# A transformer block on one core: one shared tile pool for projection, merging and feed-forward, and the first up-projection operands prepared during the last output projection

## The chip, the cores and the metric

The kernel runs as one program on one core of a Trainium2 chip. The metric is the device time of one execution in microseconds (us). Tensors are float32 in and out. The engines are named as in the profile: PE (matrix multiply, PEld its weight loads), DVE (vector), ACT (scalar and activation), POOL (GpSimd), SP (issues the DMAs). Each works through its own instruction stream in order and waits on semaphores for the others.

## The reference, cut to what matters

One encoder block on 2048 tokens of width 1024. The parts that the change touches are the last lines.

```python
h  = rmsnorm(x, norm1_g)
z  = h @ w_in + b_in                       # q, k, v, two conv inputs, two gates
br_a = neighbourhood_attention(q, k, v, rpb) @ w_na_out
br_b = silu(layernorm(dwconv31(glu))) @ w_conv_out
merged = sigmoid(g_a) * br_a + sigmoid(g_b) * br_b
x  = x + merged @ w_out                    # output projection
h2 = rmsnorm(x, norm2_g)
up = dwconv3(h2 @ w_up) + ffn_dw_b         # 1024 -> 2 * 2816
x  = x + (gelu(gate) * val) @ w_down       # 2816 -> 1024
return rmsnorm(x, norm_f_g)
```

## The kernel before, in words

Every matrix product is made at float32 accuracy out of three matmuls in a rounded 32-bit format: an operand is split into a high part (ACT copies it, line 93) and a low part (DVE subtracts the high part from it, line 94), and high x high, high x low and low x high are summed in PSUM.

Phase A (lines 663 to 733) computes the input projection, the depthwise convolution, the layer norms and the attention. Phase B (`phase_b`, lines 735 to 868) takes four quarters of 512 tokens. For each quarter `merged` makes the gated sum of the two branches in eight blocks of 128 channels (eight input tiles `Z` and eight results `M`, in sixteen `act` buffers), and then four output projections of 128 tokens follow (`tt` 0 to 3, lines 834 to 861, 48 matmuls each, written line 842). Behind each projection DVE adds the residual (line 851), SP stores x2, ACT sums the squares (line 130), POOL makes the reciprocal root in eight small operations (lines 110 to 124), and DVE scales the row (line 854). For the last two projections of quarter 3 SP stores the scaled row to `yn` (line 861).

`h2_tiles` turns finished scaled rows into the rows that the up-projection reads: PE transposes (line 891), ACT scales them (line 892), and in the odd quarters POOL makes four differences per block of channels (line 898) out of this quarter's rows and those of the quarter before, which SP loads back as `hb` (line 889). The seven combinations B11, B21, T1 to T4 and B22 go to `hc` in DRAM. The last block of tokens of quarter 3 is done later, inside the first up-projection (`h2_late`, units 4 to 7).

Phase F runs up-projection half 0, down-projection 0, up-projection half 1, down-projections 1 to 3. The up-projection uses a seven-product scheme: per pair of output blocks (a unit) seven weight combinations A11, S1, S2, A12, S3, S4, A22 (sums made by POOL at lines 955 to 963, split by ACT and DVE) meet the seven row combinations; a product is twelve matmuls (line 985). `duo` handles units 0 and 1 together, because the row combinations are loaded and split on the way: `h_tile` loads 256 KB into one of four `hraw` buffers and splits it into a tile of the `h0` to `h3` groups.

Three things order the work. In phase A the order on PE is the program's own; everywhere else the framework's scheduler places instructions into each engine's stream when their operands and buffers are due, so a load can be placed ahead of its place in the program text when its buffer is free. A tile waits for the last use of whatever lay at its address. And a pool is opened after the pool before it on the same memory has been closed: `wp` and `ap` (phases A and B) are closed before `fp` and `fps` (phase F) are opened.

```python
        with ExitStack() as outer:
            self.wp = pool(outer, "w", 2)
            self.ap = pool(outer, "act", NACT)
```

```python
            sums = [self.w_sums(self.w_raws(0)), None]
            for name in ("A11", "S1"):
                self.w_split(W[0], sums[0], name)
            build("B11")
            A.append(self.bank())
            self.product(A[0], W[0], "A11", H, "B11", first=True)
            s1.append(snap(A[0]))
            sums[1] = self.w_sums(self.w_raws(1))
            build("T1")
```

Of the kernel before, what the change touches and what calls it, by code (L numbers as in the profile page):

```python
# [12 lines left out]
F32 = mybir.dt.float32  # L13
# [35 lines left out]
NACT = 16  # L49
NRAW = 3  # L50
# [5 lines left out]
PAD_ACT, PAD_H = 256, 960  # L56
F_RAW, F_W, F_U, F_C, F_BLK, F_SNAP, F_H = 4, 9, 3, 2, 4, 5, (8, 8, 6, 6)
# [5 lines left out]
BUFS_B = {"gt": 2, "x": 4, "l": 6, "lv": 1, "h2": 3, "hb": 2, "hd": 2, "y": 1}  # L63
# [19 lines left out]
class Block:  # L83
# [12 lines left out]
    def split_weights(self, raw):  # L96
        wh = self.wp.tile([128, 8, 128], F32R, name="wh", tag="wh")
        wl = self.wp.tile([128, 8, 128], F32R, name="wl", tag="wl")
        self.split(wh, wl, raw)
        return wh, wl  # L100

    def raw(self, *shape):
        return self.wp.tile(list(shape) or [128, 8, 128], F32, name="wraw", tag="wraw", bufs=NRAW)
# [559 lines left out]
    def phase_a(self):  # L663
# [5 lines left out]
        def acts(pool, w):  # L669
            return [[pool.tile([128, w], F32R, name="act", tag="act") for _ in range(KC)] for _ in range(2)]  # L670

# [6 lines left out]
        with self.tc.manual_schedule(engines={mybir.EngineType.PE}):  # L678
            with self.pool("x0", 16) as xp, self.pool("xt", 4) as self.xt:
                self.pad(xp, PAD_ACT)  # L680
                tile = lambda: self.ap.tile([128, 1024], F32, name="act", tag="act")[:, :D]
                xs = [self.x_tiles(0, 4, tile)]
                X0 = acts(xp, 1024)
# [8 lines left out]
                for c, raw in zip((16, 12), raws):  # L692
                    w = ws[c] = [self.wp.tile([128, 8, 128], F32R, name=n, tag=n) for n in ("wh", "wl")]
# [11 lines left out]
                X1 = acts(self.ap, 1024)  # L705
# [29 lines left out]
    def phase_b(self):  # L735
# [20 lines left out]
        def load_z(qd):  # L756
# [3 lines left out]
            for src in (self.at, self.cs):  # L760
                for kc in range(4):
                    t = self.ap.tile([128, 1024], F32R, name="act", tag="act")
# [28 lines left out]
        def merged(qd, Z, M):  # L791
            for d in range(8):
# [18 lines left out]
                m = self.ap.tile([128, 1024], F32R, name="act", tag="act")  # L811
# [9 lines left out]
        def main():  # L821
# [5 lines left out]
            for qd in range(4):  # L827
                M, xs = [], []
                yield from merged(qd, Z, M)
                if qd < 3:  # L830
                    Z = load_z(qd + 1)
                load_x(qd * 4)
                load_x(qd * 4 + 1)
                for tt in range(4):
# [20 lines left out]
                    xs.append(x)  # L855
                    if tt < 2:
# [25 lines left out]
    def h2_step(self, kc, e, t0, xs, ps, st, b0, t2):  # L882
# [42 lines left out]
    def k4(self, name, tag, bufs, shape=(128, 1024), dtype=F32):  # L925
        return self.fp.tile(list(shape), dtype, name=name, tag=tag, bufs=bufs)

# [3 lines left out]
    def h_tile(self, H, half, name, kc):  # L931

        r = self.k4("hraw", "hraw", 4, (128, 512))
        self.nc.sync.dma_start(r, self.hc[half, kc, H_AT[name]])
# [3 lines left out]
        self.split(t[:, 0], t[:, 1], r)  # L938
# [10 lines left out]
    def w_sums(self, raws):  # L949

        ra, rb = raws
        s = self.k4("ws", "ws", 2, (128, 2, 4, 128))
# [14 lines left out]
    def w_split(self, W, sums, name):  # L967
        t = W[name] = self.k4("w", "w", F_W, (128, 2, 4, 128), F32R)
# [4 lines left out]
    def w_side(self, raws):  # L973

        sums, W = self.w_sums(raws), {}
# [16 lines left out]

    def phase_up(self, half):
        nc = self.nc
        H = {}
# [70 lines left out]
        def duo():  # L1066

            W, A, E, s1, s5, s2, ua, ub = [{}, {}], [], [], [], [], [], [], []
            build = lambda name: [self.h_tile(H, half, name, kc) for kc in range(4)]
            sums = [self.w_sums(self.w_raws(0)), None]  # L1070
            for name in ("A11", "S1"):
                self.w_split(W[0], sums[0], name)
            build("B11")
            A.append(self.bank())
            self.product(A[0], W[0], "A11", H, "B11", first=True)
            s1.append(snap(A[0]))
            sums[1] = self.w_sums(self.w_raws(1))
            build("T1")
            E.append(self.bank())
            self.product(E[0], W[0], "S1", H, "T1", first=True)  # L1080
            s5.append(snap(E[0]))
# [3 lines left out]
            A.append(self.bank())  # L1085
            self.product(A[1], W[1], "A11", H, "B11", first=True)
            s1.append(snap(A[1]))
            E.append(self.bank())
            self.product(E[1], W[1], "S1", H, "T1", first=True)
            s5.append(snap(E[1]))  # L1090
# [40 lines left out]

        tail = duo()
        wr = {f: self.w_raws(f) for f in (2, 3)}
        Ws = {2: self.w_side(wr.pop(2))}
        for f in range(2, NF):
            if f + 1 < NF:
                Ws[f + 1] = self.w_side(wr.pop(f + 1))
# [7 lines left out]
    def phase_down(self, g):  # L1145
# [67 lines left out]
    def layout(self):  # L1213

        unused = lambda tag, bufs, shape=(128, 1024): self.k4("place", tag, bufs, shape)
        unused("raw", F_RAW)
        unused("ws", 2)
        self.edge = self.fp.tile([128, 124, 2], F32, name="edge")
        unused("w", F_W)
        unused("snap", F_SNAP, (128, 512))  # L1220
        unused("u", F_U, (128, 1083))
        unused("c", F_C, (128, 1027))
        self.pad(self.fp, PAD_H)
        unused("hraw", 4, (128, 512))
        unused("h0", F_H[0])
# [96 lines left out]
```

## Time and profile before

| what | value |
|---|---|
| median of three runs (lowest to highest) | 2808.43 us (2805.88 to 2808.47) |
| the profiled execution's own time | 2805.53 us |
| its span, first to last instruction | 2803.7 us |
| mean granted TensorE clock | 0.989 of 2.4 GHz |
| PE busy | 2715.3 us, 97% of the span |
| DVE / ACT / POOL busy | 1886.3 / 1185.6 / 555.4 us |
| moved by DMA | 463.68 MB, mean 165 GB/s |

The profiled execution lies 1.8 us above its span and 2.9 us (0.1%) below the median. A row of a timeline gives the start and the length of a run of like instructions, the engine, the line, the operation, what it writes and reads, the count, and in brackets how long the engine had been idle and what ended that. A row of waits gives the total, the number and the longest. A window row gives for each engine the busy time and count, then the granted clock, the DMA share and the GB/s.

### The profile page before, as it was taken

Reading aid. Unit: us, or ns where it says so; the run is one execution under the profiler, and the core shown is the slowest. Engines: PE = TensorE matmul, PEld = TensorE weight load, DVE = VectorE, ACT = ScalarE, POOL = GpSimd, SP = SyncE. Lnnn points to the kernel's source line nnn. Section 1 sums busy time; section 2 is a strip of 40 time slices with the busy share of each in tenths; the row PEclk is TensorE's granted clock in tenths of the full one; section 3 lists DMA queues with packets and bytes.
Section 4 is the critical chain, followed back from the end, with each engine's and each line's share of the span. In section 5 each row is a group of like instructions: output and inputs, shape, how many; then the busy total and the mean of one; then the engine's idle time right before and its main releaser. Section 6 shows DMA issues by size and latency. Waiting matters only on the chain.

```text
span 2803.7 us, 34637 instructions
## 1 busy us (share of the span) xinstructions
PE 2715.3 (97%) x12597; PEld 2247.2 (80%) x12597; DVE 1886.3 (67%) x2636; ACT 1185.6 (42%) x1880; POOL 555.4 (20%) x731
## 2 busy tenths in 40 slices
PE   7998999999999999999969999999999999999998
PEld 6787788888888887887858788888888888888887
DVE  4697999668777646756528877875587778734252
ACT  6422222246555543422325555463454555533231
POOL 1101000000000000132043555430444344002021
PEclk9999999999999999999989999999999999999999
DMA  5357733489788868767545342236522222556361
GB/s 176 99 143 235 266 121 117 135 226 253 211 236 230 225 194 288 220 217 233 188 159 168 114 123 83 83 123 209 162 93 83 89 77 83 170 176 216 120 218 53
DMA packets 427704, 463.68 MB, mean 165 GB/s; under 512 B 27041, under 2 KB 336013, under 8 KB 426509
## 3 DMA queue, kind: packets, MB, share of 16 engines
q1 hardware_dynamic: 427533, 461.47, 52.9%
q8 instruction: 99, 1.62, 0.2%
q14 instruction: 72, 0.59, 0.1%
HBM read 336.81 MB, written 141.05 MB: 170 GB/s over the span
## 4 chain that ended last, share of the span: by engine, by line
PE 75%; DMA 9%; issue 6%; DVE 5%; POOL 2%; ACT 2%; SPq 1%; ACTq 0%; POOLq 0%; DVEq 0%
PE bank L985 26%; PE bank L1178 17%; PE mm L297 7%; PE mm L295 7%; PE mm L299 7%; PE ot L614 2%; PE s L569 2%; PE pt L595 2%; PE mm L842 1%; DMA bd<-rext 1%; DMA gt<-gs 1%; SPq L216 1%; DMA hraw<-hc 1%; DMA y<-ys 1%; PE mm L802 1%
## 5 line engine op out<-in xcount | busy, mean ns | idle before, releaser
L985 PE MATMUL bank<-h,w 128*128 128x512 f32 x3696 | 847.0, 391 | 26.2 <-ACT h L93 22.4
L985 PEld LDWEIGHTS bank<-h,w 128*128 128x128 f32 x3696 | 695.1, 188 | 174.1 <-ACT h L93 23.8
L1178 PE MATMUL bank<-wd,g 128*128 128x512 f32 x2112 | 479.7, 389 | 0.0
L295 PE MATMUL mm<-act,wh 128*128 128x512 f32 x1152 | 460.2, 399 | 14.9 <-ACT qt L342 8.7
L1178 PEld LDWEIGHTS bank<-wd,g 128*128 128x128 f32 x2112 | 396.5, 188 | 82.2
L297 PE MATMUL mm<-act,wh 128*128 128x512 f32 x1152 | 461.2, 400 | 0.0
L299 PE MATMUL mm<-act,wl 128*128 128x512 f32 x1152 | 458.4, 398 | 0.2 <-DVE wl L94 0.2
L444 DVE SCALAR_TENSOR_TENSOR acc<-u,dw,acc 128x1008 f32<-128x1008 f32 (+1 forms) x240 | 310.9, 1296 | 5.8
L94 DVE TENSOR_TENSOR w<-wraw,w 128x512 fp32r<-128x512 f32 x220 | 206.9, 953 | 106.5 <-ACT w L93 106.2
L295 PEld LDWEIGHTS mm<-act,wh 128*128 128x128 f32 x1152 | 218.7, 190 | 56.2 <-ACT qt L342 9.9
L299 PEld LDWEIGHTS mm<-act,wl 128*128 128x128 f32 x1152 | 218.8, 190 | 37.0 <-DVE wl L94 0.7
L297 PEld LDWEIGHTS mm<-act,wh 128*128 128x128 f32 x1152 | 218.6, 190 | 36.1 <-DVE act L250 0.3
L94 DVE TENSOR_TENSOR wd<-draw,wd 128x1024 fp32r<-128x1024 f32 x88 | 107.0, 1222 | 177.0 <-ACT wd L93 176.5
L93 ACT ACTIVATE w<-wraw 128x512 fp32r<-128x512 f32 x220 | 135.9, 626 | 164.7 <-PE bank L985 132.6
L93 ACT ACTIVATE wh<-wraw 128x1024 fp32r<-128x1024 f32 x102 | 107.9, 1058 | 211.1 <-PE mm L297 165.7
L93 ACT ACTIVATE wd<-draw 128x1024 fp32r<-128x1024 f32 x88 | 93.2, 1060 | 206.9 <-DMA draw<-in_w_down 151.2
L1016 DVE SCALAR_TENSOR_TENSOR c<-u,fw,c 128x1023 f32<-128x1023 f32 (+1 forms) x88 | 131.7, 1496 | 62.1 <-ACT c L1015 61.6
L94 DVE TENSOR_TENSOR wl<-wraw,wh 128x1024 fp32r<-128x1024 f32 x102 | 126.5, 1241 | 51.9 <-ACT wh L93 47.3
L842 PE MATMUL mm<-woh,act 128*128 128x512 f32 x512 | 142.8, 396 | 2.6 <-DVE gt L809 2.6
L1244 POOL MEMSET pad<- 128x1 f32 x4 | 0.4, 128 | 728.2 <-PE s L569 727.9
L1015 ACT ACTIVATE c<-u,cols,fw 128x1023 f32<-128x1023 f32 (+1 forms) x88 | 109.5, 1245 | 64.7 <-DVE c L1030 37.0
L124 POOL TENSOR_SCALAR v<-ms 128x1 f32<-128x1 f32 x36 | 10.5, 291 | 628.7 <-ACT junk L130 314.6
(169 smaller groups left out, 3831.8 us busy)
## 6 DMA issues: line engine op xcount, KB each, us to landing
wraw<-in_w_up SPq DMA_DIRECT2D x88, 512.0 KB
draw<-in_w_down SPq DMA_DIRECT2D x88, 512.0 KB
wraw<-in_w_in SPq DMA_DIRECT2D x72, 512.0 KB
graw<-gd SPq DMA_DIRECT2D x44, 512.0 KB
gs<-gate SPq DMA_DIRECT2D x64, 256.0 KB
q<-qs SPq DMA_DIRECT2D x64, 256.0 KB
v<-vs SPq DMA_DIRECT2D x128, 128.0 KB
gt<-gs SPq DMA_DIRECT2D x32, 512.0 KB
```

Of the source, the lines that this page charges most:

```text
L93: self.nc.scalar.activation(hi, src, AF.Copy)
L94: self.nc.vector.tensor_tensor(lo, src, hi.bitcast(F32), op=ALU.subtract)
L295: mm(ps, wh[:, kc], X[kc][:, 0:512], start=kc == 0, stop=False)
L297: mm(ps, wh[:, kc], X[kc][:, 512:1024], start=False, stop=False)
L299: mm(ps, wl[:, kc], X[kc][:, 0:512], start=False, stop=kc == KC - 1)
L444: tap = nc.vector.scalar_tensor_tensor(acc, u[:, k : k + n], w(k), acc, ALU.mult, ALU.add)
L569: nc.tensor.matmul(ps[:, :w], q[:, s * 512 + rt * 128 : s * 512 + rt * 128 + 128], kv[:, r0 : r0 + nr, st : st + 32], start=s == 0, stop=s ...
L842: mm(ps[:, nh], l, r[kc][:, nh * 512 : nh * 512 + 512], start=kc == 0 and l is mh and r is woh, stop=kc == KC - 1 and l is ml,)
L985: self.nc.tensor.matmul(ps, w[:, x, kc], h[:, y], start=first and kc == 0 and i == 0, stop=kc == 3 and i == 2, skip_group_check=True,)
L1015: nc.scalar.activation(c, u[:, 1 : 1 + n], AF.Identity, scale=tap(1), bias=self.col(C_FFB, ch))
L1016: nc.vector.scalar_tensor_tensor(c, u[:, 0:n], tap(0), c, ALU.mult, ALU.add)
L1178: mm(ps[tt][nh], x[:, tok], y[:, c], start=f == 0 and i == 0, stop=f == NF - 1 and i == 2,)
```

## The change

It replaces the pools `wp` and `ap` by one pool `ep` that stays open over all phases. `ep` holds four raw buffers (phases A and B had three of their own), five weight buffers `w` (before: two pairs), one buffer `ws0` for sums, and the groups `h0` and `h1` of eight tiles, which serve as the `act` tiles of phases A and B and as row tiles of the up-projection. A new generator `early` loads the raw weights of units 0 and 1 and the row combinations B11 and T1 and makes the splits that the first two products of unit 0 read; in half 0 it is stepped inside the last quarter of phase B, in half 1 it is run through at the start. The `hraw` buffers go: a row combination is loaded into the low half of its tile and split in place. The weights of a unit are divided over two groups of five, `w` and `w1`, where one group of nine served. Three of the four differences of `h2_step` become DVE operations that read PSUM, the fourth a DVE subtraction; POOL makes none. The layer-norm buffers of phase B go from six to five, and the small pads that set addresses get new sizes.

```diff
-F_RAW, F_W, F_U, F_C, F_BLK, F_SNAP, F_H = 4, 9, 3, 2, 4, 5, (8, 8, 6, 6)
+F_RAW, F_W, F_U, F_C, F_BLK, F_SNAP, F_H = 4, (5, 5), 3, 2, 4, 5, (8, 8, 6, 6)
...
-BUFS_B = {"gt": 2, "x": 4, "l": 6, "lv": 1, "h2": 3, "hb": 2, "hd": 2, "y": 1}
+BUFS_B = {"gt": 2, "x": 4, "l": 5, "lv": 1, "h2": 3, "hb": 2, "hd": 2, "y": 1}
...
+    def k4(self, name, tag, bufs, shape=(128, 1024), dtype=F32):
+        pool = self.ep if tag in ("raw", "w", "ws0", "h0", "h1") else self.fp
+        return pool.tile(list(shape), dtype, name=name, tag=tag, bufs=bufs)
+
+    def act(self, j, dtype=F32R):
+        return self.k4("act", f"h{j}", 8, dtype=dtype)
...
                 yield from merged(qd, Z, M)
+                early = self.early(0) if qd == 3 else iter(())
                 if qd < 3:
                     Z = load_z(qd + 1)
+                next(early, None)
                 load_x(qd * 4)
...
                     xs.append(x)
+                    next(early, None)
                     if tt < 2:
...
-        sub = lambda o, x, y: nc.gpsimd.tensor_tensor(o, x, y, op=ALU.subtract)
+        def less(out, e, y):
+            x = ps[:, e * 256 : e * 256 + 256]
+            nc.vector.scalar_tensor_tensor(out, x, self.col(C_G2, kc + 4 * e), y, ALU.mult, ALU.subtract)
+
         t2 = t2[:, 0]
-        sub(b0[:, 0], st[:, 0], b0[:, 0])
-        sub(t2, st[:, 1], b0[:, 0])
-        sub(st[:, 0], st[:, 1], st[:, 0])
-        sub(b0[:, 1], b0[:, 1], t2)
+        less(b0[:, 0], 0, b0[:, 0])
+        less(t2, 1, b0[:, 0])
+        less(st[:, 0], 1, st[:, 0])
+        nc.vector.tensor_tensor(b0[:, 1], b0[:, 1], t2, op=ALU.subtract)
...
-    def h_tile(self, H, half, name, kc):
-
-        r = self.k4("hraw", "hraw", 4, (128, 512))
-        self.nc.sync.dma_start(r, self.hc[half, kc, H_AT[name]])
+    def h_load(self, H, half, name, kc):
+
...
         t = H[name, kc] = self.k4("h", shape=(128, 2, 512), dtype=F32R, **self.h_tag(j))
-        self.split(t[:, 0], t[:, 1], r)
+        self.nc.sync.dma_start(t[:, 1].bitcast(F32), self.hc[half, kc, H_AT[name]])
+
+    def h_split(self, t):
+        self.split(t[:, 0], t[:, 1], t[:, 1].bitcast(F32))
...
     def w_split(self, W, sums, name):
-        t = W[name] = self.k4("w", "w", F_W, (128, 2, 4, 128), F32R)
+        j = name in ("S4", "S3", "A22")
+        t = W[name] = self.k4("w", "w1" if j else "w", F_W[j], (128, 2, 4, 128), F32R)
...
+    def early(self, half):
+
+        H, W, raws = {}, [{}, {}], [self.w_raws(f) for f in range(2)]
+        self.begun = H, W, raws, []
+        first = [(name, kc) for name in ("B11", "T1") for kc in range(4)]
+        for x in first:
+            self.h_load(H, half, *x)
+        yield
+        sums = self.w_sums(raws[0], 0)
+        self.begun[3].append(sums)
+        for name in ("A11", "S1"):
+            self.w_split(W[0], sums, name)
+        yield
+        for x in first[:4]:
+            self.h_split(H[x])
+        yield
+        for x in first[4:]:
+            self.h_split(H[x])
+        yield
...
+            def heads(i):
+                for ps, snaps, a, b in ((A, s1, "A11", "B11"), (E, s5, "S1", "T1")):
+                    ps.append(self.bank())
+                    self.product(ps[i], W[i], a, H, b, first=True)
+                    snaps.append(snap(ps[i]))
+
+            heads(0)
+            sums.append(self.w_sums(raws[1], 1))
             for name in ("A11", "S1"):
                 self.w_split(W[1], sums[1], name)
             build("T2")
...
+            heads(1)
             both = lambda name: [self.w_split(W[i], sums[i], name) for i in range(2)]
...
+        if half:
+            for _ in self.early(half):
+                pass
+        H, W, raws, sums = self.begun
         tail = duo()
...
-                    gh = self.k4("g", "w", F_W, (128, 2, 512), F32R)
-                    gl = self.k4("g", "w", F_W, (128, 2, 512), F32R)
+                    gh, gl = [
+                        self.k4("g", "w1" if j else "w", F_W[j], (128, 2, 512), F32R)
+                        for j in ((f + i) // 2 % 2 for i in range(2))
+                    ]
...
-        with ExitStack() as outer:
-            self.wp = pool(outer, "w", 2)
-            self.ap = pool(outer, "act", NACT)
-            self.pad(self.ap, PAD_ACT)
...
+        self.ep = pool(ctx, "shared", 1)
```

## Rows read from the trace of the kernel before

**Rows 1.** PE's waits, whole run: total us, times, longest us.

```profile
PE bank L985 <- ACT h L93: 22.4, 3, 19.8
...
PE mm L806 <- DVE wl L94: 3.1, 4, 1.9
...
PE bank L985 <- DVE h L94: 2.8, 3, 2.4
...
PE bank L891 <- DMA late<-yn: 2.5, 1, 2.5
```

**Rows 2.** PE's timeline between output projection and up-projection.

```profile
1438.85 0.60 PE L891 MATMUL pt<-ident,x 128*128 128x128 f32 x4
1459.25 3.88 PE L985 MATMUL bank<-h,w 128*128 128x512 f32 x7 [19.80 <-ACT h L93]
...
1483.56 46.77 PE L985 MATMUL bank<-h,w 128*128 128x512 f32 x205 [0.22 <-DVE h L94]
```

**Rows 3.** Groups by form, 1439 to 1530 us: busy, mean ns, idle before.

```profile
L985 PE MATMUL bank<-h,w 128*128 128x512 f32 x263 | 65.6, 409 | 25.3 <-ACT h L93 22.4 <-DVE h L94 2.8
...
L94 DVE TENSOR_TENSOR h<-hraw,h 128x512 fp32r<-128x512 f32 x28 | 22.6, 832 | 9.4 <-ACT h L93 9.3
...
L93 ACT ACTIVATE h<-hraw 128x512 fp32r<-128x512 f32 x28 | 17.1, 626 | 15.5 <-DMA hraw<-hc 15.0
...
L955 POOL TENSOR_TENSOR ws<-wraw 128x512 f32<-128x512 f32 x6 | 9.5, 1580 | 21.2 <-DMA wraw<-in_w_up 19.0 <-DVE w L94 2.1
```

**Rows 4.** The chain that ended last: start us, us, what.

```profile
1439.07 2.64 DMA hb<-hc
...
1476.84 5.29 DMA hraw<-hc
...
1628.87 261.40 PE bank L985 x1153
```

**Rows 5.** Windows: PE, PEld, DVE, ACT, POOL busy; clock, DMA share, GB/s.

```profile
1250.00:1316.00 66.00, 58.10 (x257) 46.12 (x256) 46.11 (x70) 19.59 (x31) 20.19 (x33) 0.97 0.87 264
...
1394.00:1440.00 46.00, 45.45 (x208) 37.31 (x207) 9.95 (x10) 7.34 (x15) 12.71 (x32) 1.00 0.20 75
...
1440.00:1450.00 10.00, 0.00 (x0) 0.00 (x0) 0.27 (x1) 1.25 (x3) 7.55 (x16) 0.62 0.67 237
...
1460.00:1465.00 5.00, 4.06 (x10) 2.12 (x9) 5.00 (x4) 2.38 (x4) 4.84 (x4) 0.72 1.16 326
...
1623.00:1642.00 19.00, 19.00 (x87) 15.72 (x87) 15.53 (x16) 10.54 (x16) 10.69 (x12) 1.00 0.47 144
```

**Rows 6.** SP's timeline: one hoisted load, and the end of phase B.

```profile
1377.11 0.82 SPq L788 DMA_DIRECT2D x<-in_x  x2
...
1450.97 0.32 SPq L861 DMA_DIRECT2D yn<-x  x1
1451.34 1.50 SPq L945 DMA_DIRECT2D wraw<-in_w_up  x2
```

**Rows 7.** SP's own waits, 1370 to 1530 us: total us, times, longest.

```profile
SPq L934 <- DVE h L94: 27.2, 23, 3.2
```

**Rows 8.** ACT's timeline: the last sum of squares of phase B.

```profile
1441.27 0.19 ACT L130 ACTIVATION_READ_ACCUMULATOR mm<-x 128x1 f32 x1
```

**Rows 9.** POOL's timeline: a reciprocal root from first to last, and a waiting difference.

```profile
1217.93 0.19 POOL L124 TENSOR_SCALAR v<-ms 128x1 f32<-128x1 f32 x1 [9.62 <-ACT mm L130]
...
1220.63 0.27 POOL L114 TENSOR_SCALAR r<-rt,r 128x1 f32<-128x1 f32 x1
...
1281.27 2.41 POOL L898 TENSOR_TENSOR hb<-h,hb 128x256 f32<-128x256 f32 x2 [13.44 <-DMA wraw<-in_w_conv_out]
```

**Rows 10.** DVE's timeline: a PSUM operation of 128x256, and two weight splits.

```profile
53.44 0.48 DVE L250 SCALAR_TENSOR_TENSOR act<-pt,cols,act 128x256 fp32r<-128x256 f32 x1 [1.36 <-ACT act L249]
...
1267.14 1.76 DVE L94 TENSOR_TENSOR wl<-wraw,wh 128x1024 fp32r<-128x1024 f32 x1
...
1272.55 1.22 DVE L94 TENSOR_TENSOR wl<-wraw,wh 128x1024 fp32r<-128x1024 f32 x1
```

More of the change, by code (lines that the diff above doesn't have):

```diff
@@ L96, in split_weights @@
     def split_weights(self, raw):
-        wh = self.wp.tile([128, 8, 128], F32R, name="wh", tag="wh")
-        wl = self.wp.tile([128, 8, 128], F32R, name="wl", tag="wl")
+        wh, wl = [self.k4("w" + x, "w", F_W[0], (128, 8, 128), F32R) for x in "hl"]
         self.split(wh, wl, raw)
@@ L102, in raw @@
     def raw(self, *shape):
-        return self.wp.tile(list(shape) or [128, 8, 128], F32, name="wraw", tag="wraw", bufs=NRAW)
+        return self.k4("wraw", "raw", F_RAW, shape or (128, 8, 128))
+    def k4(self, name, tag, bufs, shape=(128, 1024), dtype=F32):
[3 more added lines that the diff above has]
+        return self.k4("act", f"h{j}", 8, dtype=dtype)
     def col(self, base, i):
@@ L679, in phase_a @@
             with self.pool("x0", 16) as xp, self.pool("xt", 4) as self.xt:
-                self.pad(xp, PAD_ACT)
-                tile = lambda: self.ap.tile([128, 1024], F32, name="act", tag="act")[:, :D]
+                self.pad(xp, PAD_X)
+                tile = lambda: self.act(0, F32)
                 xs = [self.x_tiles(0, 4, tile)]
-                X0 = acts(xp, 1024)
+                X0 = [[xp.tile([128, 1024], F32R, name="act", tag="act") for _ in range(KC)] for _ in range(2)]
                 ws = {}
@@ L692, in phase_a @@
                 for c, raw in zip((16, 12), raws):
-                    w = ws[c] = [self.wp.tile([128, 8, 128], F32R, name=n, tag=n) for n in ("wh", "wl")]
+                    w = ws[c] = [self.k4(n, "w", F_W[0], (128, 8, 128), F32R) for n in ("wh", "wl")]
                     with self.tc.issue_after(self.his[0]) if c == 12 else nullcontext():
@@ L704, in phase_a @@
                     pass
-                X1 = acts(self.ap, 1024)
+                X1 = [[self.act(b) for _ in range(KC)] for b in range(2)]
                 def half1():
@@ L1066, in duo, with build @@
         def duo():
[L1068 to L1081, printed above, removed]
+            A, E, s1, s5, s2, ua, ub = [], [], [], [], [], [], []
+            def build(name):
+                for kc in range(4):
+                    self.h_load(H, half, name, kc)
+                for kc in range(4):
+                    self.h_split(H[name, kc])
+            def heads(i):
[5 more added lines that the diff above has]
+            sums.append(self.w_sums(raws[1], 1))
             for name in ("A11", "S1"):
@@ L1215, in layout @@
         unused = lambda tag, bufs, shape=(128, 1024): self.k4("place", tag, bufs, shape)
-        unused("raw", F_RAW)
-        unused("ws", 2)
-        self.edge = self.fp.tile([128, 124, 2], F32, name="edge")
[L1219 to L1225, printed above, removed]
+        self.pad(self.fp, PAD_G)
+        unused("w1", F_W[1])
+        unused("ws1", 1)
+        self.pad(self.fp, PAD_H)
+        for j in (2, 3):
+            unused(f"h{j}", F_H[j])
+        self.edge = self.fp.tile([128, 124, 2], F32, name="edge")
         self.gf = self.fp.tile([128, D], F32, name="gf")
-        for j in (3, 1, 2):
-            unused(f"h{j}", F_H[j])
     def phase_f(self):
-        self.up = self.a["w_up"][0].rearrange("(k p) c -> p k c", p=128)
         self.layout()
@@ L1270, in run @@
         self.sp = pool(ctx, "small", 5)
[L1271 to L1287 removed]
+        self.ep = pool(ctx, "shared", 1)
+        self.up = self.a["w_up"][0].rearrange("(k p) c -> p k c", p=128)
+        for tag, n in (("raw", F_RAW), ("w", F_W[0]), ("ws0", 1)):
+            self.k4("place", tag, n)
+        self.pad(self.ep, PAD)
+        for j in range(2):
+            self.k4("place", f"h{j}", 8)
+        with ExitStack() as c:
+            self.pp = _Psum(pool(c, "psa", 1, space=PSUM), {"mm": 2, "s": 2, "pt": 2, "ot": 2})
+            self.tp, self.tags, self.bufs = pool(c, "ta", 1), TAGS_A, BUFS_A
+            self.cvp = pool(c, "conv", 1)
+            self.phase_a()
+        with ExitStack() as c:
+            self.pp = _Psum(pool(c, "psb", 1, space=PSUM), {"mm": 2, "s": 2, "pt": 2})
+            self.tp = pool(c, "tb", 1)
+            self.yp = [lambda: self.T([128, 4, 128], name="y")] * 2
+            self.tags, self.bufs = TAGS_B, BUFS_B
+            self.wop = pool(c, "wo", 1)
+            self.pad(self.wop, PAD_WO)
+            self.phase_b()
         with ExitStack() as c:
```

44 lines of the change are left out of this document (9 added, 35 removed).

## Prediction, made before the changed kernel was run

> **What bounds the kernel now.** I read PE's waits over the whole run first: PE is busy almost throughout (the table above), so only its stops can be won. One stands out, 19.8 us before a product of line 985 that waits for a split row tile, with 2.6 us more on the same line and 2.8 us on the low parts [rows 1]. PE's timeline puts it at the seam between phase B and the up-projection: the last transposes end at 1439.45 us, the next matmul starts at 1459.25 [rows 2]. I then read who is late there. SP issues the first up-projection load at 1451.34, directly behind the store of the last scaled row, which DVE finished only then [rows 6]; the loads stand behind the closing of phase B's pools. After that the row tiles trickle: SP stands 27.2 us, 23 times, waiting for a split to free an `hraw` buffer [rows 7].
>
> The size of the loss: from 1439.45 to the end of the run that ends at 1530.33 there are 263 up-projection matmuls [rows 2, 3]. At the steady pace, 261.40 us for 1153, or 0.2267 us each [rows 4], they need 59.6 us and took 90.9. The loss is **31.3 us**: 25.3 us is idle time [rows 3], the other 6.0 us is matmuls at a lower clock: granted 0.62 on the mean of the first ten empty us, so part at 2.4 and part at 1.2 GHz, and 0.72 from 1460 to 1465, after PE had stood still [rows 5].
>
> **The change part by part.** *Early operands.* Four weight loads of 512 KB and eight row loads of 256 KB (4.2 MB), four POOL sums, ten ACT high parts and ten DVE low parts leave the seam. They go beside the last output projections, where in 46 us DVE works 9.95, ACT 7.34, POOL 12.71 and the DMA share is 0.20 [rows 5]. They need about 10 x 0.63 = 6.3 us on ACT, 10 x 0.83 = 8.3 on DVE, 4 x 1.6 = 6.4 on POOL [rows 3], and at 237 GB/s [rows 5] some 18 us of DMA. That is covered. Without the cover the residual rows would be late, but SP already places such loads ahead of their place in the text (x rows at 1377, in the middle of merging) [rows 6]. The row tiles B11 and T1 take the eight `Z` buffers, free when merging ends near 1394, so they can land by about 1412, 27 us before use. I cost this at 0.
>
> *The new seam.* Unit 0's two first products (24 matmuls, 5.44 us) start at 1439.45 and end at 1444.9; unit 1's A11 product, its weights being raw, ends at 1447.6. Its S1 product needs two POOL sums, now placed after the pools change. The last sum of squares ends at 1441.46 [rows 8]; without differences in between the root takes 2.97 us from first to last [rows 9], so POOL is free at about 1444.5 (in the trace the differences interleave with it and push the last row to 1450.94). Two sums of 1.58 us and one high part of 0.63 [rows 3] give 1448.3: a stop of about **1 us** with its low part. Next come T2's four rows. DVE's last scaling (0.75 us) and the store allow SP the first load at about 1445.6; a landing takes between 2.64 us (a small load here) and 5.29 us (a row tile with the queue full) [rows 4], so with the splits T2 is ready between 1449.5 and 1455, against PE's need at 1451.3. I take **1 us**, nearer the short end, since the queue is then nearly empty. After that 16 more row tiles and the weights of units 2 and 3 (6.3 MB) are due within some 27 us, 233 GB/s; between 237 and 326 GB/s were moved in this stretch [rows 5]. SP no longer stands for `hraw`. I take **1 us** more. The remainder is 3 us of 31.3, a gain of **28 us**. Bounds: nothing waits (31 us), or T2 comes as late as the loads came before, issued at 1451.0 and landed and split 7 us later, PE waiting from 1451.3 and again for the 4 us that a late queue adds, 11 us in all (gain 20).
>
> *Differences on DVE.* POOL loses 64 subtractions, DVE gains 48 operations on PSUM and 16 subtractions of 128x256. The nearest row, the same operation and shape from PSUM, is 0.48 us [rows 10]: 31 us more on DVE in all, of them 15 in quarter 1 and the merging after it. There DVE works 46.11 of 66 us and PE already loses 7.9 us [rows 5]. Two things pull apart. Weight splits that ran while POOL made differences took 1.76 us, the same split otherwise 1.22 [rows 10], and PE waited 3.1 us for such low parts [rows 1]. Against that, a difference waits for `hb`, and what stood behind it on POOL was little; on DVE it is the weight split, the gate product, the residual. POOL once stood 13.44 us before a difference whose rows were loaded back [rows 9]. I take **0**, with -3 and +10 us as ends: below, the split waits vanish; above, most of one such wait reaches PE.
> The trace alone leaves open whether POOL caused the long splits. The Trainium skill (SBUF — State Buffer, Who interferes with whom) says that a DVE operation with two SBUF inputs contends with a POOL operation that reads SBUF, one with a single SBUF input does not. By that rule the new PSUM operations would be free of it and the sum would be 3 us lower; by the row alone it stays as it is.
>
> In units 4 to 7 four operations, 1.9 us, join DVE's 15.5 of 19 us [rows 5]: 17.4, still under PE's 19. Cost 0; if that cover failed, +3 us over four units. The 2.5 us wait for `late` [rows 1] is neither moved nor mended.
>
> *The rest.* Larger raw and weight buffers in phases A and B lie on no wait of PE over 3.1 us [rows 1]: 0, bounds -2 and +2. Five layer-norm buffers for six: 0, because a norm has several output blocks of time; +2 if not. Half 1's start had no stop at all before, its loads lie in the down-projection: 0, up to +3 if the four raw buffers are taken too soon.
>
> **Sum.** The profiled execution's 2805.5 less 28 is 2777.5. It lies 2.9 us under the median, so I put the changed kernel's median between the two, at **2779 us**.
>
> **Rivals.** *The stop moves behind the fourth product.* PE runs through the four prepared products and stops for T2 and the S1 sums, because SP and POOL are still bound to phase B's tail. For it: both stand behind the last row in strict order. Against: the tail itself gets shorter without POOL's differences. Worked out above as 11 us left: 2805.5 - 20 = 2785 to 2788.
> *DVE becomes the limit of phase B.* The waits for `hb` move to DVE. For it: the 13.44 us wait [rows 9] and 7.9 us already lost. Against: DVE has 20 us free in that stage. Price 10 to 13 us of the 28: 2788 to 2791.
> *Slower: the two weight groups starve the units.* One group of nine served seven tiles of a unit, the last of the unit before and one spare; now four of `w` and three of `w1` have five buffers each. If S3 and S4 of the next unit come free too late, PE waits in every one of some 40 units. From 0.7 us per unit the gain of 28 is gone; at 1 us the time is 2805.5 - 28 + 40 = 2818. Against: in the order of the products each of these buffers comes free at least five products (13.6 us) before its successor is read, as with nine; PE ran 1153 matmuls there without a gap [rows 4].
> *It does not do what it says.* The early loads are placed behind the tail after all, as all of phase F was: 2805, no change.
>
> **How the numbers follow.** Forecast 0.63, the moved stop 0.16, DVE as limit 0.09, starved units 0.06, no effect 0.05, and 0.01 elsewhere. The likeliest case spans 2769 (31 us at the seam, 5 from the splits and buffers) to about 2785; with the next two it reaches to 2798 (20 us at the seam, 12 or so given back), which leaves out about 0.15. Faster means by over 0.2% (5.6 us, about what a measurement of this kernel tells from no change): 0.63 + 0.16 + 0.09, and 0.01; within 0.2%: 0.05; slower: 0.06.
>
> **What would show it.** Right: up-projection loads and splits between 1375 and 1415; the first line 985 matmul within 1 us of the last transpose; no stop over 2 us in the next 60 us and a granted clock of 1.00 throughout; no wait of SP for a row tile's split. Wrong: an idle PE after four products with T2 or a POOL sum as releaser; DVE idle ahead of a line of `h2_step` with PE's waits on `wl` or `gt` over 5 us in quarter 1; repeated waits of line 985 for `w` tiles in units 2 to 21. The prediction fails outright if the seam still shows a stop over 12 us.

## The result, and the profile after

The changed kernel takes **2791.09 us** (median of four runs, 2787.22 to 2791.60), the kernel before beside it 2807.33 (four, 2805.88 to 2808.47): a ratio of **0.9939**, 95% interval 0.9922 to 0.9957. Run again later (after_again below) it took 2793.25 (five runs, 2791.58 to 2795.36) against 2803.26 (nine), 0.9964 (0.9951 to 0.9978). It is faster, by 10 to 16 us. The forecast was 2779, a gain of 28.

The profiled execution has an own time of 2787.22 us and a span of 2785.4. From the list of PE's matmuls, cut at four events:

| stretch | before | after | difference |
|---|---|---|---|
| start to the first merging matmul | 1042.9 | 1044.9 | +2.0 |
| merging and output projections | 396.1 | 394.1 | -2.0 |
| end of the last output projection to the start of the 240th up-projection matmul | 85.7 | 70.3 | **-15.4** |
| from there to PE's end | 1268.6 | 1266.0 | -2.5 |

The first line says nothing: over the thirteen profiles after the first it lies between 1039.4 and 1047.7, with the same code there. Nor does the second: in the twelve of them that make the differences on DVE it lies between 392.6 and 400.1. So single whole times say little here, and the experiments are read by the third line, called **the seam** below. (A product of a weight block and a row block is twelve matmuls: the fourth product begins with the 37th. Where the expectations count 36 or 240 products, single matmuls are meant.) At PE's steady 0.2267 us [rows 4] 239 matmuls take 54.2 us. The seam has lost 31 us before (the prediction's 31.3) and 16 after: half is won.

PE's waits over the whole run, after, which answer to [rows 1]:

```profile
PE mm L803 <- DVE gt L810: 9.5, 4, 3.2
PE bank L991 <- DVE h L904: 8.3, 1, 8.3
...
PE bank L991 <- DVE w L92: 2.0, 1, 2.0
...
PE mm L845 <- DVE gt L810: 1.7, 2, 1.5
```

PE's timeline at the seam, after, answering to [rows 2]:

```profile
1440.92 0.44 PE L895 MATMUL pt<-ident,x 128*128 128x128 f32 x2 [0.71 <-ACT h L896]
1441.11 3.00 PE L991 MATMUL bank<-h,w 128*128 128x512 f32 x12
1452.42 7.23 PE L991 MATMUL bank<-h,w 128*128 128x512 f32 x24 [8.31 <-DVE h L904]
1460.75 1.25 PE L991 MATMUL bank<-h,w 128*128 128x512 f32 x4 [1.10 <-ACT w L91]
1464.02 81.00 PE L991 MATMUL bank<-h,w 128*128 128x512 f32 x356 [2.01 <-DVE w L92]
```

The 19.8 us stop is gone. The first product starts behind the last transposes. The second waits 8.3 us for a difference on DVE: it writes the PSUM bank which that difference still reads (f1_bank_free below shows it). The fourth (S1 of unit 1) waits 1.1 and 2.0 us for its split. In the 356 matmuls from 1464.02 on there is no stop.

The clock in windows of that stretch (PE busy, then the granted clock), answering to [rows 5]:

```profile
1441.00:1445.00 4.00, 3.11 (x14) 1.00 0.78 210
...
1452.00:1456.00 4.00, 3.58 (x9) 0.54 0.96 311
...
1464.00:1468.00 4.00, 3.98 (x17) 1.00 0.54 214
```

In the window after the 8.3 us stop PE was granted 0.54, near the lower level of 1.2 GHz, and from 1456 on 1.00, which is 2.4 GHz. The DMA share is 0.96 in that window.

The chain of waits through the seam, after, as in [rows 4]:

```profile
1441.38 5.92 DMA h<-hc
1447.32 0.64 ACT h L91
...
1450.97 0.41 DVE hb L904
...
1453.61 0.48 SPq L914
...
1454.83 3.30 DMA h<-hc
...
1462.21 1.77 DVE w L92
```

So the bound is now a tail: row loads and their splits, then the last differences, their stores, and one more row load. What each engine did first and what it did behind that shows in the timelines of SP, POOL and ACT (one fence each):

```profile
1429.00 0.32 SPq L940 DMA_DIRECT2D h<-hc  x1
...
1440.39 1.39 SPq L940 DMA_DIRECT2D h<-hc  x3
1441.87 0.38 SPq L893 DMA_DIRECT2D hb<-hc  x1
...
1453.61 0.48 SPq L914 DMA_DIRECT2D hc<-hb  x1
1454.19 6.71 SPq L940 DMA_DIRECT2D h<-hc  x12
```

```profile
1457.39 1.29 POOL L960 TENSOR_TENSOR ws<-wraw 128x512 f32<-128x512 f32 x1 [11.80 <-DMA hc<-h]
```

```profile
1458.40 0.63 ACT L91 ACTIVATE h<-h 128x512 fp32r<-128x512 f32 x1 [9.93 <-DMA h<-hc]
...
1460.07 1.15 ACT L91 ACTIVATE w<-wraw 128x512 fp32r<-128x512 f32 x2
```

T2's and also T4's rows, both in the shared pool's `h1`, were hoisted into the output projection (1429.00 to 1440.39), that is, the scheduler placed their loads ahead of their place in the program; T4's last three stand ahead of a load of old rows (`hb`) that the last differences need. Unit 1's first sum waited 11.8 us for a store. Its tile `ws1` lies in the pool that opens behind phase B, where the `h2` tiles lay that the store reads: in e9_s1 below, which moves it by exchanging two lines of the layout, the same sum starts at 1445.06 and not at 1457.39. And ACT waited 9.9 us at the split of B21's first row, with S1's split behind it. B21's rows themselves had been stored by 1178 us; what kept them was SP's order and their space, which opens behind the last stores.

### The profile page after: what moved, and what is told of

Read it like the earlier page. It is cut to its first block, busy times and chain, and to the rows that moved or that the text cites. A ratio compares the mean times of both kernels' runs of the same rounds, so it can differ in the third digit from the quotient of the medians.

```text
span 2785.4 us, 34643 instructions
## 1 busy us (share of the span) xinstructions
PE 2709.3 (97%) x12597; PEld 2244.6 (81%) x12597; DVE 1913.3 (69%) x2700; ACT 1187.0 (43%) x1880; POOL 518.7 (19%) x668
## 4 chain that ended last, share of the span: by engine, by line
PE 81%; DMA 10%; DVE 3%; issue 2%; SPq 1%; ACT 1%; POOL 1%; ACTq 0%; DVEq 0%; POOLq 0%
PE bank L991 29%; PE bank L1206 17%; PE mm L301 7%; PE mm L299 7%; PE mm L303 7%; PE mm L845 4%; PE ot L618 2%; PE s L573 2%; DMA bd<-rext 2%; PE pt L599 2%; PE mm L803 1%; PE mm L805 1%; PE mm L807 1%; SPq L220 1%; DMA gt<-gs 1%
## 5 line engine op out<-in xcount | busy, mean ns | idle before, releaser
L991 PE MATMUL bank<-h,w 128*128 128x512 f32 x3696 | 843.5, 390 | 11.4 <-DVE h L904 8.3
L92 DVE TENSOR_TENSOR w<-wraw,w 128x512 fp32r<-128x512 f32 x220 | 190.8, 883 | 21.3 <-ACT w L91 21.2
L92 DVE TENSOR_TENSOR w<-ws,w 128x512 fp32r<-128x512 f32 x88 | 84.3, 960 | 82.8 <-ACT w L91 82.7
L1040 ACT ACTIVATE c<-u,cols,fw 128x1023 f32<-128x1023 f32 (+1 forms) x88 | 109.6, 1245 | 72.7 <-DVE c L1055 55.1
```

Source lines behind the costliest of these rows:

```text
L92: self.nc.vector.tensor_tensor(lo, src, hi.bitcast(F32), op=ALU.subtract)
L991: self.nc.tensor.matmul(ps, w[:, x, kc], h[:, y], start=first and kc == 0 and i == 0, stop=kc == 3 and i == 2, skip_group_check=True,)
L1040: nc.scalar.activation(c, u[:, 1 : 1 + n], AF.Identity, scale=tap(1), bias=self.col(C_FFB, ch))
```

## The experiments

Single profiles unless a median is given. The figures, in us after the last output projection's end:

| run | 37th up-projection matmul (fourth product) starts | 240th starts (the seam) |
|---|---|---|
| before | 37.5 | 85.7 |
| after, again | 21.8, 21.4 | 70.3, 72.7 |
| e1_bank | 21.9 | 73.2 |
| e2_pool | 21.6 | 70.4 |
| e5_noearly | 22.0 | 70.5 |
| f1_bank_free | 21.4 | 70.9 |
| e9_s1, e10_s1bank | 23.6, 23.2 | 69.6, 69.2 |
| e3_hold_t4 | 19.7 | 70.0 |
| f2_bank_s1 | 15.7 | 69.0 |
| f4_hb_early | 11.9 | 63.6 |
| h3_all | 16.2 | 64.8 |
| i1_all | 10.3 | 61.5 |

Four of these profiles have the same order of work at the seam and gave 70.3, 72.7, 73.2 (e1_bank) and 70.5 (e5_noearly). So a difference of less than 3 us between two single profiles decides nothing.

The theories are: **bank** (the 8.3 us stop is the loss), **queues** (several things of unit 1 stand behind phase B's tail, and lifting one only moves the stop), **DVE order** (the differences were better on POOL), **hoisted loads** (T4's loads make the tail late), and whether the shared pool or the new place in the text lets the work run early.

**The second product's bank.**

```diff
+            free = [self.bank() for _ in range(6)]
...
-                    ps.append(self.bank())
+                    ps.append(free.pop(0 if ps is A and i == 0 else 2))
```

> The changed kernel, but the second up-product writes into a PSUM bank that the last transposes did not use, so its 8.3 us stop for the DVE difference has no reason left. Measure: the time from the end of the last output projection (1438.98 in the changed kernel) to the 240th up-product, 70.3 us there and 85.7 before. Theory 'bank': that stop is the loss, so the figure falls by 7 to 8 us to about 62, and the time to about 2779. Theory 'queues': all work of the second unit's fourth product waits anyway for sums whose space the last stores hold until 1457.4 and for splits that stand on ACT behind the split of B21's first rows (1458.4); the second and third product run at 1444 to 1450, the stop moves ahead of the fourth product and is as much longer, the figure stays at 69 to 70.5 and the time within 1.5 us of 2787 to 2791.

This run doesn't test the theory: the stop stayed, at 8.7 us for the same difference, so the second product still had its old bank. (That banks are given out in the order of first use explains it, but no view shows it directly.) As a second profile of the same seam it gave 73.2 (the clock: see the end). The edit that does move the bank is in the transposes:

```diff
-            ps = self.pp.tile([128, 512], F32, name="pt", tag="s")
+            ps = self.pp.tile([128, 512], F32, name="pt", tag="pt" if t0 >= 1536 else "s")
```

> The changed kernel with the last transposes in the other pair of PSUM banks, so that the second and third product write banks without a late reader; the fourth product now gets the bank of the last difference. (In the run e1_bank the second product still had its old bank, since banks are handed out in the order of first use.) Theory 'bank': the 8.3 us stop goes and 240 products end 62 us after the last output projection. Theory 'queues': 36 products run without a stop, then the fourth waits some 11 to 13 us for the split of the second unit's S1, which stands behind B21's first two splits on ACT: 69 to 70.5 us, as in the changed kernel (70.3).

PE's timeline of f1_bank_free (its last row, and that of e2_pool below, ends at the end of the window, not at a stop):

```profile
1445.38 8.44 PE L991 MATMUL bank<-h,w 128*128 128x512 f32 x36
1464.55 2.08 PE L991 MATMUL bank<-h,w 128*128 128x512 f32 x4 [10.72 <-ACT w L91]
1466.99 18.19 PE L991 MATMUL bank<-h,w 128*128 128x512 f32 x71 [0.37 <-DVE w L92]
```

36 matmuls, three products, run without a stop, then PE stands 10.7 us for S1's split. The seam is 70.9: the largest wait of the seam was worth nothing by itself. "Bank" falls.

**The differences back on POOL.**

```diff
-        def less(out, e, y):
...
+        sub = lambda o, x, y: nc.gpsimd.tensor_tensor(o, x, y, op=ALU.subtract)
```

> The changed kernel with the four differences of each row tile back on GpSimd, from SBUF copies, as before the change. Theory 'DVE order' (the differences stand behind the splits of T2 and T4 on DVE, and this is what makes the last stores late): the stores come 3 to 5 us earlier and so do B21's rows; 65 to 67 us from the last output projection to the 240th product. Theory 'queues': the loads of T4 still stand ahead of the last two loads of the old rows (hb), so the differences can't start before about 1445 and take 8 x 0.72 us on GpSimd to about 1451; 69.5 to 72 us.

Here the differences read copies in SBUF and no longer the bank, and the picture is that of f1_bank_free: 36 matmuls, then a stop. PE's timeline of e2_pool:

```profile
1436.54 8.44 PE L989 MATMUL bank<-h,w 128*128 128x512 f32 x36
1457.67 22.64 PE L989 MATMUL bank<-h,w 128*128 128x512 f32 x87 [12.70 <-ACT w L91]
```

The seam is 70.4, so "DVE order" falls too.

**Unit 1's sums and S1's split alone**, with the second product's old bank (e10_s1bank adds e1's edit, which does nothing, and so repeats e9_s1):

```diff
-        unused("w1", F_W[1])
         unused("ws1", 1)
+        unused("w1", F_W[1])
...
+                    with self.tc.issue_after(s1_split.ins) if half == 0 and name == "B21" else nullcontext():
                         self.h_split(H[name, kc])
```

> The changed kernel with two edits: the sums of the second unit lie in the space of the gate tiles (free since 1390) and not in that of the last differences' tiles, and B21's splits come after the split of the second unit's S1 on ACT and DVE. The second product's bank is as it was. Theory 'queues': the GpSimd sums run at about 1445.5 to 1449, S1 is split by about 1454, so after the 8.3 us stop (to 1452.4) 36 products run without a stop; the next limit is B21's rows, loaded behind the last stores (issued at 1454.2, split by about 1463). The span from the last output projection to the 240th up-product falls from 70.3 to 65 to 68 us. Theory 'bank': nothing happens (70 us), since the 8.3 us stop stays.

> Both: the two edits on the second unit's sums and splits, and the free bank for the second product. Theory 'queues': products one to three run on from 1441, the fourth starts at about 1454, and B21's rows (loaded behind the last stores) limit from about 1463: 63.5 to 66 us from the last output projection to the 240th product, that is 4 to 7 us less than the changed kernel, and 1 to 2 less than with the sums and splits alone. Theory 'bank': 62, as with the bank alone.

The seams are 69.6 and 69.2, less of a gain than "queues" expected and within the spread. PE stood once, 10.4 us for the bank, and 384 matmuls followed without a stop. With **both** wait points lifted, f1_bank_free's edit and e9_s1's together:

> The run before plus the two edits of e9_s1 (the second unit's sums in the gate tiles' space, its S1 split ahead of B21's splits). Theory 'queues': the 10.4 us stop of e9_s1 is gone, since neither bank nor sums hold anything before the fourth product; that starts at about 1454 (its split on DVE follows the last difference), B21's rows limit from about 1463: 62.5 to 66 us to the 240th product, 4 to 7 less than e9_s1 (69.6). Theory 'each stop is its own': no more than the 0.7 us that e9_s1 gained; 69 us.

PE's timeline of f2_bank_s1:

```profile
1436.18 8.44 PE L992 MATMUL bank<-h,w 128*128 128x512 f32 x36
1449.71 1.19 PE L992 MATMUL bank<-h,w 128*128 128x512 f32 x2 [5.08 <-DVE h L905]
1451.15 7.12 PE L992 MATMUL bank<-h,w 128*128 128x512 f32 x22 [0.25 <-DVE w L92]
1460.40 78.34 PE L992 MATMUL bank<-h,w 128*128 128x512 f32 x336 [2.13 <-ACT w L91]
```

The fourth product starts 6 us earlier than in the changed kernel, and almost all of it is given back: a stop for S2's split, which now stands behind B21's first splits (ACT waited 9.2 us there), and two stretches at half clock (0.50 at 1449 to 1452, 0.58 at 1462 to 1466). The seam is 69.0 where 62.5 to 66 was expected: a miss of 3 us, with the next wait in the line where "queues" put it, at B21's rows.

**T4's loads held**, and nothing else:

```diff
+        with self.tc.issue_after(self.hb_load.ins) if half == 0 and name in ('T4',) else nullcontext():
+            self.nc.sync.dma_start(t[:, 1].bitcast(F32), self.hc[half, kc, H_AT[name]])
```

> The changed kernel, with T4's loads held on SP behind the last load of old rows, and nothing else. Theory 'hoisted loads' (T4's loads and splits, hoisted into the output projection because the shared pool is open there, put the tail's differences late): differences end at about 1446 to 1448 and not 1452.6, stores and B21's rows come 4 to 5 us earlier, 65 to 67 us to the 240th product. Theory 'old rows' (the loads of old rows wait for the stores of the tiles that they reuse, T4's place changes nothing): within 1 us of 70.3.

PE's stop before the second product falls from 8.3 to 3.3 us, so T4's loads do hold the differences; but the fourth product's stop grows to 5.5, and the seam is 70.0. So the cause that the theory names is real, but it gains nothing alone.

**The old rows early**, added to f2_bank_s1:

```diff
+            first = "hb" if t0 < HALF else "sq"
...
-            b0, t2 = (self.T([128, n, 256], name=x) for n, x in ((2, "hb"), (1, "hd"))) if t0 // 512 % 2 else (None, None)
+            b0, t2 = (self.T([128, n, 256], name=x) for n, x in ((2, first), (1, "hd"))) if t0 // 512 % 2 else (None, None)
```

> The run before plus one: in the last quarter the tiles for the loaded old rows (hb) come from the group of five layer-norm tiles and not from the group of two, so that no load of old rows waits for a store or stands behind T4's loads. Theory 'queues': differences of the last two row tiles at about 1440 to 1445 and not 1448.6 to 1452.6, the stores and B21's rows some 5 us earlier, one or two short stops of 1 to 2 us left: 58 to 61 us from the last output projection to the 240th product, time 2775 to 2781. Rival 'rows are enough': B21 isn't the limit, the figure stays within 1 us of the run before.

The seam is 63.6: 5.4 us better than f2_bank_s1 and the largest single step, though 2.6 over its range. The rival (within 1 us) falls. 3 us of it were lost again later: from the 240th matmul to PE's end it took 1269.5, where the others took 1265.7 to 1266.7, and PE waited 3.7 us for `late` there (0.8 in the changed kernel). This edit alone, without the other two, was not run, so it isn't shown how much of the 5.4 us needs them.

**The shared pool or the place in the text.**

```diff
-                early = self.early(0) if qd == 3 else iter(())
+                early = iter(())
...
-        if half:
-            for _ in self.early(half):
-                pass
+        for _ in self.early(half):
+            pass
```

> The changed kernel, but the early part (first weights' and rows' loads, sums and splits) stands in the text at the start of the up-projection and not between the tiles of the last output projection. Theory 'shared pool': what lets the work run early is that its tiles lie in a pool that is open in both phases; the planner hoists it by itself, first product at 2 us after the last output projection and 240 products at 69.5 to 71.5 us, as in the changed kernel (70.3). Theory 'place in the text': the first product starts 10 to 20 us later and the figure is 80 to 86, as in the kernel before (85.7).

The seam is 70.5, with the same three stops. The steps written between the tiles of the output projection do nothing that the scheduler doesn't do by itself. What is left is that the tiles lie in a pool that is open in both phases; that follows by exclusion, as no run had this kernel with divided pools. It would also be why T4's loads ran early though nobody asked for it.

**All together.** To f4_hb_early, B21 gets T4's place in the shared pool:

```diff
-H_PLACE = ("B11", "T1", "T2", "T4", "B21", "B22", "T3")
+H_PLACE = ("B11", "T1", "T2", "B21", "B22", "T3", "T4")
```

> The changed kernel with all that held the seam taken away together: the last transposes in the other PSUM banks, the second unit's sums in the gate tiles' space, its S1 split ahead of B21's splits, the last quarter's old rows (hb) in the layer-norm group, and B21 in the place of T4 in the shared pool, so that B21's and not T4's rows are loaded during the output projection. Theory 'queues': in the run f4_hb_early the stop that was left (2.4 us and then some 6 us at half clock) came from S1's split on DVE behind T4's splits and from B21's rows behind the last stores; both go, the fourth product starts at about 11 us after the last output projection, and 240 products take 57.5 to 60.5 us from its end (63.6 there, 70.3 in the changed kernel). Of the 10 to 13 us gained on the changed kernel at the seam at least 7 stay to the end: 2777 to 2784 us against 2791, ratio to the kernel before 0.989 to 0.992. Rival 'rows limit later': B22, T3 and T4, now all loaded behind the last stores, stop the eighth or tenth product, and the figure stays at 62 to 64.

The seam is 64.8, a miss, and the time 2785.95 (six runs, 2779.61 to 2791.93), ratio 0.9939 (0.9924 to 0.9954): no better than the change itself as far as this shows. In ACT's timeline two splits wait 7.0 us for rows, ahead of S1's:

```profile
1451.60 1.15 ACT L91 ACTIVATE h<-h 128x512 fp32r<-128x512 f32 x2 [7.04 <-DMA h<-hc]
1452.66 1.14 ACT L91 ACTIVATE w<-wraw 128x512 fp32r<-128x512 f32 x2
```

They are B22's, whose loads were issued from 1447.66 on and whose splits the scheduler had moved up once B21's were held. Holding these too, `name in ("B21", "B22")`:

> The run h3_all, with B22's splits also held behind the split of the second unit's S1. In h3_all two of B22's splits came to stand ahead of S1's on ACT and waited for rows that are loaded behind the last yn store (to 1451.6, a stop of 5.6 us, then 4 us at half clock). Theory 'queues': S1 is split on ACT at about 9.5 us after the last output projection and on DVE behind the last x scaling (10 to 12.5 us), so the stop shrinks to 1 to 3 us and 240 products end 60 to 62 us after the last output projection (64.8 there, 70.3 in the changed kernel). Rival 'transfers' (the DMA rings are full from 1434 to 1448, B21 and B22 come no earlier whatever the order of the engines): the stop moves behind the fourth or the eighth product and the figure stays at 63.5 to 65. The whole time is 2777 to 2784 us by the first.

PE's and then DVE's timeline of i1_all:

```profile
1444.22 9.36 PE L993 MATMUL bank<-h,w 128*128 128x512 f32 x40
1455.86 31.15 PE L993 MATMUL bank<-h,w 128*128 128x512 f32 x129 [2.28 <-DVE w L92]
```

```profile
1452.99 1.61 DVE L858 TENSOR_SCALAR x<-x,r 128x1024 f32<-128x1024 f32 x1 [5.25 <-DMA x<-x]
1454.53 0.68 DVE L92 TENSOR_TENSOR w<-ws,w 128x512 fp32r<-128x512 f32 x1
1455.13 1.28 DVE L92 TENSOR_TENSOR w<-wraw,w 128x512 fp32r<-128x512 f32 x2
```

The seam is 61.5, as expected, and the fourth product starts at 10.3. **2781.11 us** (four runs, 2778.20 to 2782.25), ratio **0.9918** (0.9904 to 0.9932). On the same chip, against the same runs of the kernel before, the change itself:

> The changed kernel itself, on the same chip and against the same runs of the kernel before as i1_all. Theory 'queues': 70 to 71 us from the last output projection to the 240th product, whatever the time before it, and a ratio to the kernel before of 0.993 to 0.995; i1_all is 6 to 10 us shorter than this. Rival 'noise of the first phases': the two medians differ by less than 4 us.

2793.25 and 0.9964 (0.9951 to 0.9978): the intervals lie apart, and i1_all beats both kernels, by 22 us and 12. Of the 12, 11.1 are at the seam (72.7 to 61.5; 72.7 itself is over its range, by the clock; from the 70.3 of the first profile it is 8.8). "Noise" falls. What the last two steps add to f4_hb_early is not decided: its seam of 63.6, h3_all's 64.8 and i1_all's 61.5 lie within the spread.

The stop of 2.3 us that is left: S1's low part stands on DVE behind the last x scaling, and that waits for the store of x before it may overwrite it. The store was issued at 1444.97 and is done at about 1452.9, in windows whose DMA share is 0.84 and 0.92. That transfers limit here is thus read off a timeline, not tested: neither another tile for the scaled row nor less to transfer was tried.

## Why the prediction was right and wrong

**Right: sign, place and mechanism.** The loss was the seam, the first operands were ready in time, and the first product starts 0.2 us after the start of the last two transposes. The early part was hidden as costed (0): the loads, sums and splits of A11, S1, B11 and T1 were done by 1403, and SP waits for no split of a row tile there.

**Wrong: the remainder of the new seam, 3 us, measured 16** (13.7 when counted, as there, from the end of the last transposes). It had three terms.
- "Two sums of 1.58 us and one high part of 0.63 give 1448.3: a stop of about 1 us." POOL came free at 1445.6, an us later than forecast, but the sums started at 1457.39. The term counted who computes them and not where they are written: `ws1` lies in the space of the last stores' tiles. Nor did it ask what stands ahead of S1's split on ACT: B21's. Lifting both (e9_s1) gained 0.7 us, within the spread, as the bank stopped PE all the same, and the bank had no term at all. The kernel before could not show it: there the last use of a PSUM tile of phase B, by ACT's sum of squares, ends at 1441.46 [rows 8], long before the first product at 1459.25 [rows 2].
- T2's rows, 1 us: there is no such wait. Its loads went out from 1429.0 to 1434.7, not from 1445.6, and its splits were done by 1439.3.
- Sixteen more row tiles, 1 us: no stop after 1464.02, so 0.

The nearest case was the first rival (stop after four prepared products, 11 us left, 2785 to 2788). It had the right cause, SP and POOL still bound to phase B's tail, but put the stop a product late (behind three products, and with the bank behind one), and the cost 5 us low. Neither case had a term for the clock, and the rival's 4 us "that a late queue adds" rest on no row. Of the 16 us, 11.4 are idle before products, about 2 the clock at 0.54 in one window, and 2.4 pass before the last transposes end (0.4 in the kernel before), with 1.06 us of waits for ACT. The measured 2791 lies outside the likeliest case (up to 2785) and inside the whole range only by the room that the rivals took. That it falls on the price of "DVE becomes the limit" (2788 to 2791) is luck: what is missing of the 28 us was lost at the seam.

**Differences on DVE (0, -3 to +10)** came out near 0, but not by the two ends that were weighed. An operation takes 0.472 to 0.478 us on the median, as [rows 10] had it. The stage from 1040 to 1440 took 394.1 us after 396.1, and 392.5 in e2_pool with the differences on POOL again; against the spread of 392.6 to 400.1 one profile decides nothing there. PE's waits for `wl` [rows 1], the low end, are gone, but in e2_pool they are gone too. So the move of the differences didn't end them; what did is open (five weight buffers for two pairs is a candidate that no run tests). Of the high end a part did come: PE's waits for `gt` rose from 4.0 to 11.2 us in that stage, and lie between 9.9 and 14.7 in all twelve runs with the differences on DVE. Three of those in the changed kernel, 6.0 us, stand in and behind the merging of quarter 2, where differences of quarter 1 are made (PE's timeline, then DVE's):

```profile
1281.09 0.50 PE L803 MATMUL mm<-act,wh 128*128 128x512 f32 x1 [2.57 <-DVE gt L810]
...
1291.58 0.53 PE L803 MATMUL mm<-act,wh 128*128 128x512 f32 x1 [2.02 <-DVE gt L810]
...
1310.81 0.70 PE L845 MATMUL mm<-woh,act 128*128 128x512 f32 x2 [1.46 <-DVE gt L810]
```

```profile
1279.82 1.22 DVE L810 SCALAR_TENSOR_TENSOR gt<-gt,mm 128x1024 f32<-128x1024 f32 x1 [3.47 <-DMA gt<-gs]
...
1290.21 1.22 DVE L810 SCALAR_TENSOR_TENSOR gt<-gt,mm 128x1024 f32<-128x1024 f32 x1 [2.30 <-DMA gt<-gs]
```

So DVE wasn't short of time there: it stood idle for a load of `gt`. In e2_pool PE has no wait for `gt` in that place, and 5.0 us over its whole run (PE's waits):

```profile
PE mm L803 <- DVE gt L810: 3.7, 2, 3.5
...
PE mm L845 <- DVE gt L810: 1.3, 1, 1.3
```

That the differences on DVE are what makes these loads late is likely by this, but rests on one profile.

Eleven of the differences from PSUM ran beside a sum of POOL (three each in e9_s1, e10_s1bank and f2_bank_s1, two in f4_hb_early) and took 0.470 to 0.484 us, no longer than without. The Trainium skill (SBUF — State Buffer, Who interferes with whom) says that an operation of DVE with at most one SBUF input, outside the 2-port modes, does not contend with POOL; the traces agree.

**DVE as limit of phase B, starved units, no effect**: of the signs named for the first, over 5 us of waits for `gt` did show (6.0 us, above), but DVE stood idle for loads of `gt` and not ahead of a line of `h2_step`, and the price of 10 to 13 us was not paid. Its 13.44 us wait [rows 9] is put down by the row to a load of raw weights; that the old rows were what it waited for is a reading which the row doesn't bear out. Units weren't starved: PE's waits of the whole run name no `w` tile outside the seam. **The rest (0)** gave -2.5: PE's wait for `late` fell from 2.5 to 0.8 us, and a snap's wait went. The prediction said that this wait is not mended; the loads came earlier all the same.

## What to carry to other kernels

When work is moved across a phase boundary, list for each of its instructions four things: who computes it, what stands ahead of it in that engine's order, what last used the space that it writes (tile and PSUM bank), and what its loads wait behind. Here several such holds covered the same stretch, and the largest one in the waits was worth nothing until others went: f1_bank_free removed 8.3 us of wait and gained none, i1_all left one stop of 2.3 us before the fourth product and gained 9 to 11. And opening space to the scheduler moves more than was meant, so look at what else it hoists.

## What the runs showed of the hardware

**The clock after a short stop is not the same from run to run.** After the same 2.0 us stop the changed kernel went on at a granted 1.00 (above), e1_bank at 0.50 and 0.73. Windows of e1_bank:

```profile
1462.00:1466.00 4.00, 3.70 (x9) 0.50 0.80 313
1466.00:1470.00 4.00, 4.00 (x15) 0.73 0.48 132
1470.00:1474.00 4.00, 4.00 (x19) 1.00 0.79 226
```

after_again shows the same, 0.50 and 0.69, and the two seams are 73.2 and 72.7 for 70.3. From the first product to the 240th matmul PE stood 11.4 us in the changed kernel and in e1_bank alike, so the longer seam is the clock. So one 2 us stop costs 2 or 5 us, and that is the spread that a single profile has here.

**DVE beside POOL.** The last x scaling took 1.61 us in i1_all, while POOL ran a sum from 1452.78 to 1454.06; the other scalings there have a median of 0.75. In all profiles together seven scalings ran beside a sum or a difference of POOL and took 1.19 to 1.80 us, and none of the others took over 0.76. In f4_hb_early two splits took 2.90 us together beside POOL's sums, where one is 0.68 alone. The Trainium skill (SBUF — State Buffer, Who interferes with whom) says that a scaling of this kind can enter a mode that takes the ports shared with POOL, and that two SBUF inputs contend with POOL's reads. The traces agree; they don't show which mode ran.
